# A hybrid mixer's convolution, recurrence and output projection in another order: one tile convolved by token halves, the gating by channel halves, the recurrence started one tile later

## The chip, the cores and the metric

One core of one Trainium2 chip runs the whole layer in a single program. The metric is the device time of one execution in microseconds (us). Before the change the median of three runs is 857.23 us (855.66 to 857.37). Five units of the core matter here: TensorE (PE in the rows; its weight loads are PEld) multiplies, VectorE (DVE), ScalarE (ACT) and GpSimd (POOL) work on elements, and SyncE (SP) issues most DMAs. Each works through its own list of instructions in order and waits where an input of the next instruction is not there.

## The reference

A decoder layer on 512 tokens of width 1024: a half-step feed-forward network, a mixer, another half-step feed-forward network, each behind an RMS norm and added to the stream. All is float32. The change lies in the mixer, which has a convolution branch (`u`) and a recurrence branch (`yr`) of 512 channels each:

```python
z = h @ w_in
c_val, c_gate, r_x, r_gate = jnp.split(z, [W_CONV, 2 * W_CONV, 2 * W_CONV + W_LRU], axis=-1)
u = c_val * jax.nn.sigmoid(c_gate)
u = causal_depthwise_conv(u, conv_dw, conv_dw_bias)          # 31 taps along the tokens
u = jax.nn.silu(layernorm(u, conv_ln_g, conv_ln_b))          # over the 512 channels
xr = causal_depthwise_conv(r_x, lru_conv_w, lru_conv_b)      # 4 taps
yr = rg_lru(xr, lru_w_a, lru_b_a, lru_w_x, lru_b_x, lru_lambda)
yr = yr * jax.nn.gelu(r_gate, approximate=True)
return jnp.concatenate([u, yr], axis=-1) @ w_out
```

In `rg_lru`, two sigmoid gates r and i are block-diagonal products of xr, a = exp(-8 r softplus(-lambda)), and h[t] = a[t] h[t-1] + sqrt(1 - a[t]^2) i[t] xr[t].

## The kernel before

Channels lie on the 128 partitions and the 512 tokens along the free axis, so each branch has four channel tiles, c = 0 to 3. To keep float32 accuracy, operands of the large products are split into a high and a low part (`hi`, `lo`), and each product takes three passes: hi by hi, hi by lo, lo by hi.

The kernel is a list of units, and each unit issues the matrix products of one weight slab. `run` walks through the list; after every 2.72 us of products it lets generators that stand beside the list (`chains`, `convs`, `pool_convs`) issue some of their steps, by a clock that it keeps in its head for each engine. A scheduler then orders each engine's instructions by priorities (`PR_CONV` is low, `PR_LN` high) and by the order in which they were issued. What it made stands fast: it is each engine's list.

The mixer's units, in order:

- `zc_units(c)`: gate and value columns of convolution tile c. `val_out` (L650) multiplies value by sigmoid(gate) and writes the input of the convolution. Tiles 0 and 1 come in two token halves, A (tokens 0 to 255) and B, tiles 2 and 3 whole. The order is 0A, 1A, 0B, 1B, tile 2, then `rx_units` (the recurrence's four input tiles, with their 4-tap convolution on VectorE at L775), then tile 3, then `rg_units` (the recurrence's four gate tiles; their Gelu at L799 waits for the key `roots`).
- The 31-tap convolution: tiles 0, 2 and 3 run on VectorE (`conv_dve`: 31 tap instructions into two PSUM accumulators and one addition, L691 to L701), tile 1 on GpSimd and ScalarE (`conv_pool`). `val_out` starts it when a tile's last token is there. Each finished tile adds a product with a matrix of ones to a bank `pm` (`channel_sum`, L677): the mean over channels. After the fourth, `layernorm` runs: subtraction of the mean (L731), squares (L736), a second `channel_sum` for the variance, square root (L740), reciprocal, scaling, Silu, split into `uhi` and `ulo` (L746 to L757).
- `lru`, the recurrence: eight float32 products `pga` with their sigmoids (L815, L816), tanh, exp and squares on ScalarE (L825 to L830), a VectorE step (L833), square roots and GpSimd products (L837, L838), four scans along the tokens (L845), then for both channel halves q = 0, 1 the product with the Gelu (L852), `yhi` (L853) and `ylo` (L854). It is started when the fourth `rx` tile is evacuated, and the gating waits until no VectorE convolution is left:

```python
            if c == 3:
                chains.append((PR_LRU, lru()))
```
```python
        while "gl" not in done or convs:
            yield 1
```

- `out_units`: the output projection. For each of four token tiles, 24 products with the `y` rows (`po<-hl,yhi` and `ylo`, L557 to L559), and after all of them the `u` rows. A unit for token tile 3 stands behind a wait for the variance.

Of the kernel before, what the change touches and what calls it, by code (L numbers as in the profile page):

```python
# [13 lines left out]
P = 128  # L14
# [61 lines left out]
def layer_kernel(ctx: ExitStack, tc, x, gains, w_g1, w_u1, w_d1a, w_d1b, w_in,  # L76
# [559 lines left out]
    def zc_units(c, parts):  # L636
# [12 lines left out]
        def val_out(t0, n):  # L649
            V.tensor_mul(mx["ub"][:, c, 30 + t0:30 + t0 + n], box["v"][:, :n], box["s"][:, :n])  # L650
            dve(0.7)
            if t0 + n == T:
                if c == 1:
                    pool_convs.append(conv_pool(c))
                else:
                    convs.append(conv_dve(c))
# [16 lines left out]
    def channel_sum(key, c, v):  # L673
        if key not in pm:
            pm[key] = [bank("pm"), 0]
        ps, n = pm[key]
        PE.matmul(ps, ones, v, start=n == 0, stop=n == 3)  # L677
        pm[key][1] += 1

    def conv_done(c):  # L680
        channel_sum("mean", c, conv_out(c))
        if pm["mean"][1] == 4:
            chains.append((PR_LN, layernorm()))


    def conv_dve(c):
        acc, o = [bank("pc"), bank("pc")], conv_out(c)
        for j in range(TAPS):
            src, to = mx["ub"][:, c, j:j + T], acc[j % 2]
# [6 lines left out]
            else:  # L696
                V.scalar_tensor_tensor(out=o if j == TAPS - 2 else to, in0=src,  # L697
                                       scalar=par(c, P_DW + j), in1=to,
                                       op0=ALU.mult, op1=ALU.add)
            yield 0.66  # L700
        V.tensor_add(o, acc[0], o)  # L701
        yield 0.66
        conv_done(c)
# [21 lines left out]
    def layernorm():  # L725
        mu = pm["mean"][0]
        sq = {}
        yield 1
        for c in range(4):
# [3 lines left out]
            if c % 2 == 0:  # L733
                sq[c // 2] = slot([P, 2, T], "sq")
            s = sq[c // 2][:, c % 2, :]
            S.activation(s, v, AF.Square)  # L736
            channel_sum("var", c, s)
        yield 1
        rs = sp.tile([P, T], F32, name=nm("rs"), tag="sg", bufs=2)
        S.activation(rs, pm["var"][0], AF.Sqrt, bias=lneps)  # L740
# [3 lines left out]
        half = [slice(0, HT), slice(HT, T)]  # L744
        for i, sl in enumerate(half):
# [8 lines left out]
        for i, sl in enumerate(half):  # L754
            for c in range(4):
                v, o = conv_out(c)[:, sl], hi[c // 2][:, c % 2, sl]
                V.tensor_sub(lo[c // 2][:, c % 2, sl], v, o.bitcast(F32))  # L757
            dve(1.6)
# [4 lines left out]
    def rx_units():  # L763
# [6 lines left out]
        def evac(c):  # L770
# [8 lines left out]
            if c == 3:  # L779
                chains.append((PR_LRU, lru()))  # L780
# [7 lines left out]
    def rg_units():  # L788
# [7 lines left out]
        def evac(c):  # L796
# [3 lines left out]
            if c == 3:  # L800
# [372 lines left out]
```

## Time and profile before

| | us |
|---|---|
| median of three runs | 857.23 (855.66 to 857.37) |
| the profiled execution | 858.1 |
| its span, first to last instruction | 856.1 |
| TensorE busy | 839.2 |
| VectorE busy | 636.7 |
| ScalarE busy | 424.7 |
| GpSimd busy | 89.5 |

The profile is of one execution; all times in rows are us from the start of its span. Where several instructions of one kind follow each other, a row of the timeline gives the first one's start, the time to the last one's end, and `xN` for their number; in brackets stands how long the engine was idle before, and what ended that. An instruction's own duration overlaps the start of the next, so the distance from start to start is the cost of one in a row of many. "Chain of waits" is the chain that ended last, followed back from the end. [...]

### The profile page before, as it was taken

What the parts mean: (1) busy time and instruction counts of PE and PEld (TensorE: products, weight loads), DVE (VectorE), ACT (ScalarE), POOL (GpSimd) and SP (SyncE); (2) the same over time, 40 slices, a digit from 0 to 9 for tenths busy, and PEclk for the clock granted to TensorE, in tenths of its full rate; (3) what the DMA queues carried; (4) which work ended last, traced back from release to release, by engine and by line L of the source; (5) the groups of instructions that cost most, each with busy time, mean ns of one, the idle gap of its engine ahead of it and who ended that gap; (6) DMA issues with size and microseconds to landing.
All of it is one profiled execution on the core that took longest, in us unless ns stands there. A gap on an engine that the chain in (4) does not pass through costs nothing.

```text
span 856.1 us, 13844 instructions
## 1 busy us (share of the span) xinstructions
PE 839.2 (98%) x5612; PEld 762.9 (89%) x5612; DVE 636.7 (74%) x899; ACT 424.7 (50%) x677; POOL 89.5 (10%) x112
## 2 busy tenths in 40 slices
PE   9999999999999999999995999999999999999996
PEld 8999988999889998998783889999889998899985
DVE  4989757998657983569988569896547994558844
ACT  6746534666425662435742535555215654136623
POOL 2000010000110001109820010000000000000001
PEclk9999999999999999999998999999999999999999
DMA  7547896555985569655451021334313335223302
GB/s 255 180 148 244 298 321 220 180 190 173 309 329 180 192 248 365 224 206 187 148 182 64 4 96 50 100 122 136 113 50 100 114 114 168 74 74 99 119 30 99
DMA packets 36723, 139.14 MB, mean 163 GB/s; under 512 B 5042, under 2 KB 5170, under 8 KB 33971
## 3 DMA queue, kind: packets, MB, share of 16 engines
q1 hardware_dynamic: 29170, 112.04, 38.5%
q0 software_dynamic: 6912, 25.17, 7.7%
q8 instruction: 44, 0.72, 0.4%
q10 hardware_dynamic: 576, 1.05, 0.3%
q14 instruction: 21, 0.16, 0.1%
HBM read 110.98 MB, written 27.26 MB: 161 GB/s over the span
## 4 chain that ended last, share of the span: by engine, by line
PE 93%; DVE 4%; ACT 1%; DMA 0%; issue 0%; POOLq 0%; SPq 0%; POOL 0%; ACTq 0%
PE px L331 25%; PE pz L331 12%; PE pd L557 8%; PE pd L558 8%; PE pd L559 8%; PE pz L316 7%; PE pw L331 6%; PE pgate L316 3%; PE pup L316 3%; DVE pc L697 2%; PE po L557 2%; PE po L558 2%; PE po L559 2%; PE ptr L369 1%; PE pdl L559 1%; PE pdl L558 1%
## 5 line engine op out<-in xcount | busy, mean ns | idle before, releaser
L215 DVE TENSOR_TENSOR hl<-raw,hl 128x1024 fp32r<-128x1024 f32 (+1 forms) x132 | 139.9, 1062 | 44.2 <-ACT hl L206 31.3
L215 DVE TENSOR_TENSOR hl<-tt,hl 128x1024 fp32r<-128x1024 f32 x78 | 95.0, 1217 | 32.8 <-ACT hl L242 19.0
L331 PE MATMUL px<-sx,hl 128*128 128x256 f32 x936 | 118.8, 276 | 0.0
L331 PE MATMUL pz<-sx,hl 128*128 128x256 f32 x936 | 118.8, 276 | 0.0
L557 PE MATMUL pd<-hl,act 128*128 128x512 f32 x304 | 118.6, 390 | 0.0
L558 PE MATMUL pd<-hl,act 128*128 128x512 f32 x304 | 118.4, 389 | 0.0
L559 PE MATMUL pd<-hl,act 128*128 128x512 f32 x304 | 118.3, 389 | 0.0
L331 PEld LDWEIGHTS px<-sx,hl 128*128 128x128 f32 x936 | 111.9, 188 | 0.0
L331 PEld LDWEIGHTS pz<-sx,hl 128*128 128x128 f32 x936 | 111.9, 188 | 0.0
L331 PE MATMUL px<-h_hi,hl 128*128 128x256 f32 x630 | 97.0, 277 | 0.0
L242 ACT CAST hl<-tt 128x1024 fp32r<-128x1024 f32 x78 | 81.9, 1052 | 24.5 <-PE pd L559 18.4
L331 PEld LDWEIGHTS px<-h_hi,hl 128*128 128x128 f32 x630 | 83.7, 188 | 1.4 <-DVE um L529 0.7
L242 ACT CAST hl<-raw 128x1024 fp32r<-128x1024 f32 x78 | 65.2, 836 | 37.1 <-PE pd L559 26.3
L206 ACT CAST hl<-raw 128x1024 fp32r<-128x1024 f32 x54 | 56.0, 1051 | 50.5 <-PE pd L559 39.7
L559 PEld LDWEIGHTS pd<-hl,act 128*128 128x128 f32 x304 | 57.1, 188 | 11.9
L558 PEld LDWEIGHTS pd<-hl,act 128*128 128x128 f32 x304 | 57.1, 188 | 11.5
L557 PEld LDWEIGHTS pd<-hl,act 128*128 128x128 f32 x304 | 57.1, 188 | 11.4
L316 PE MATMUL pz<-h_hi,hl 128*128 128x512 f32 (+2 forms) x322 | 64.8, 350 | 0.0
L316 PEld LDWEIGHTS pz<-h_hi,hl 128*128 128x128 f32 x322 | 51.7, 188 | 9.2 <-issue 1.9
L697 DVE SCALAR_TENSOR_TENSOR pc<-sx,ch,pc 128x512 f32<-128x512 f32 x84 | 56.9, 747 | 0.0
L300 DVE TENSOR_TENSOR slo<-sraw,shi 128x1024 fp32r<-128x1024 f32 x24 | 29.3, 1221 | 33.7 <-ACT shi L299 33.7
L299 ACT CAST shi<-sraw 128x1024 fp32r<-128x1024 f32 x24 | 25.3, 1052 | 49.0 <-DMA sraw<-in_w_in 26.0
(182 smaller groups left out, 1348.1 us busy)
## 6 DMA issues: line engine op xcount, KB each, us to landing
raw<-in_w_g SPq DMA_DIRECT2D x44, 512.0 KB, 3.4
raw<-in_w_u SPq DMA_DIRECT2D x44, 512.0 KB, 4.3
hl<-wsi SPq DMA_DIRECT2D x16, 1024.0 KB, 4.9
sraw<-in_w_in SPq DMA_DIRECT2D x16, 512.0 KB, 6.3
wsi<-shi POOLq DMA_DIRECT2D x16, 512.0 KB, 4.2
wsi<-slo POOLq DMA_DIRECT2D x16, 512.0 KB, 5.3
raw<-in_w_d1a SPq DMA_DIRECT2D x16, 512.0 KB, 4.6
raw<-in_w_d2a SPq DMA_DIRECT2D x16, 512.0 KB, 3.5
```

The source lines that it names most:

```text
L206: return S.copy(s.hi, s.raw)
L215: ins = V.tensor_sub(s.lo, s.raw, s.hi.bitcast(F32))
L242: S.copy(s.hi, s.raw)
L299: S.copy(hi, raws[-1])
L300: V.tensor_sub(lo, raws[-1], hi.bitcast(F32))
L316: ins = PE.matmul(ps[:, c0:c1], w[:, k, :], h[:, k, t0 + c0:t0 + c1], start=(i == 0 and k == 0), stop=(i == 2 and k == KT - 1))
L331: PE.matmul(ps[:, c0:c1], w[:, k * P:(k + 1) * P], h[:, k, c0:c1], start=(first and i == 0 and k == 0), stop=(i == 2 and k == 3), skip_gro ...
L369: ins = PE.transpose(pt[:, k, :], xs[0][:, (hf * 4 + k) * P:(hf * 4 + k + 1) * P], ident)
L557: PE.matmul(ps, ahi, whi, start=first, stop=False)
L558: PE.matmul(ps, ahi, wlo, start=False, stop=False)
L559: PE.matmul(ps, alo, whi, start=False, stop=last)
L697: V.scalar_tensor_tensor(out=o if j == TAPS - 2 else to, in0=src, scalar=par(c, P_DW + j), in1=to, op0=ALU.mult, op1=ALU.add)
```

## The change

It does four things.

- `conv_dve` takes a token range. Tile 0, which arrives in halves, is convolved half by half, in 64 instructions on 256 tokens in place of 32 on 512; it starts behind 0A in place of 0B. Tiles 2 and 3 stay whole.
- The mean over channels is no longer gathered tile by tile. GpSimd adds the first three tiles (two additions, L685 and L686), and `mean`, a unit of its own among the output projection's, issues two products with the matrix of ones in place of four.
- `lru` is started by `val_out` of convolution tile 3, behind the products of that tile, in place of by the fourth `rx` tile, ahead of them; more of its ScalarE work is kept in program order.
- The recurrence is scanned and gated by channel halves. For q = 0 and then q = 1: two scans, the product with the Gelu as soon as that half's Gelu is there, `yhi`, `ylo`. It no longer waits for the last convolution. `out_units` begins with the rows of half 0 for token tiles 0 and 1, then half 1 for tile 0, then `mean`, then half 1 for tile 1, then tile 2, the wait for the variance, tile 3.

```diff
         def val_out(t0, n):
...
-            if t0 + n == T:
-                if c == 1:
-                    pool_convs.append(conv_pool(c))
-                else:
-                    convs.append(conv_dve(c))
+            if c != 1:
+                convs.append(conv_dve(c, t0, n))
+            elif t0 + n == T:
+                pool_convs.append(conv_pool(c))
+            if c == 3:
+                chains.append((PR_LRU, lru()))
...
     def conv_done(c):
-        channel_sum("mean", c, conv_out(c))
-        if pm["mean"][1] == 4:
-            chains.append((PR_LN, layernorm()))
+        done["conv", c] = True
+        if c < 3 and all(("conv", i) in done for i in range(3)):
+            pm["s"] = slot([P, T], "cs")
+            G.tensor_add(pm["s"], conv_out(0), conv_out(2))
+            G.tensor_add(pm["s"], pm["s"], conv_out(1))
+
+    def mean():
+        need(("conv", 3))
+        pm["mean"] = channel_sum([pm["s"], conv_out(3)])
+        chains.append((PR_LN, layernorm()))
...
-    def conv_dve(c):
-        acc, o = [bank("pc"), bank("pc")], conv_out(c)
+    def conv_dve(c, t0, n):
+        if t0 == 0:
+            accs[c] = [bank("pc"), bank("pc")]
+        acc, o, at = accs[c], conv_out(c), slice(t0, t0 + n)
+        us = 0.66 if n == T else 0.42
         for j in range(TAPS):
-            src, to = mx["ub"][:, c, j:j + T], acc[j % 2]
+            src, to = mx["ub"][:, c, t0 + j:t0 + j + n], acc[j % 2][:, at]
...
-            if c == 3:
-                chains.append((PR_LRU, lru()))
...
-        for c in range(4):
-            at = (slice(None), c % 2, slice(None))
-            pin(V.tensor_tensor_scan(th[c // 2][at], r[c // 2][at], xr[c // 2][at],
-                                     0.0, ALU.mult, ALU.add))
-            dve(1.2)
-        while "gl" not in done or convs:
-            yield 1
         hi, lo = two("yhi", F32R), two("ylo", F32R)
         for q in range(2):
+            for c in (2 * q, 2 * q + 1):
+                at = (slice(None), c % 2, slice(None))
+                pin(V.tensor_tensor_scan(th[c // 2][at], r[c // 2][at], xr[c // 2][at],
+                                         0.0, ALU.mult, ALU.add))
+                dve(1.2)
+            while ("gl", 2 * q + 1) not in done:
+                yield 1
             pin(V.tensor_mul(th[q], th[q], lr["gl"][q]))
...
-        out_ = [Unit(sy, 5.44, lambda t=t: part((t,), sy, "y", True)) for t in range(3)]
+        out_ = [Unit(sy, 5.44, lambda: part((0, 1), sy, ("y", 0), True, (0, 1))),
+                Unit(sy, 2.72, lambda: part((0,), sy, ("y", 1), True, (2, 3))),
+                Unit([], 0.0, mean),
+                Unit(sy, 2.72, lambda: part((1,), sy, ("y", 1), True, (2, 3)))]
+        out_ += [Unit(sy, 2.72, lambda oh=oh: part((2,), sy, ("y", 1), True, halves=(oh,)))
+                 for oh in range(2)]
```

What it does to the engines' lists shows at three places. Line numbers of the changed kernel differ by some: L710 and L714 are its convolution taps and addition, L827 the `pga` products, L845 the VectorE step of the recurrence (L833 before), L859 the scans, L864 and L866 the gating and `ylo`.

TensorE, around the fourth convolution tile's value columns. Before, where `pz_4442` is that tile's gate and `pz_4512` its value:

```order
L316 MATMUL pz_4442<-h_hi,hl_4242 128x512 x8
L815 MATMUL pga_4473<-xr_4244,bd 128x512
L815 MATMUL pga_4476<-xr_4244,bd 128x512
L815 MATMUL pga_4479<-xr_4244,bd 128x512
L815 MATMUL pga_4482<-xr_4244,bd 128x512
L815 MATMUL pga_4489<-xr_4245,bd 128x512
L815 MATMUL pga_4492<-xr_4245,bd 128x512
L815 MATMUL pga_4495<-xr_4245,bd 128x512
L815 MATMUL pga_4498<-xr_4245,bd 128x512
L316 MATMUL pz_4512<-h_hi,hl_4292 128x512 x8
```

TensorE at the same place after, where `pz_4512` is the value of that tile again and `pz_4550` the recurrence's first gate tile:

```order
L316 MATMUL pz_4512<-h_hi,hl_4329 128x512 x8
L316 MATMUL pz_4550<-h_hi,hl_4376 128x512 x8
L316 MATMUL pz_4550<-h_lo,hl_4376 128x512 x8
L316 MATMUL pz_4550<-h_hi,hl_4376 128x512 x8
L827 MATMUL pga_4581<-xr_4275,bd 128x512
L827 MATMUL pga_4584<-xr_4275,bd 128x512
L827 MATMUL pga_4587<-xr_4275,bd 128x512
L827 MATMUL pga_4590<-xr_4275,bd 128x512
L827 MATMUL pga_4605<-xr_4276,bd 128x512
```

The recurrence's products have moved behind two more units. They stood ahead of the tile's value and now stand behind it and behind one gate tile.

VectorE, from the recurrence's step on `th` to the first taps of convolution tile 3. Before (`pc` are accumulators, `sx` the convolution's input):

```order
L701 TENSOR_TENSOR cv_4324<-pc_4322,cv_4324 128x512
L650 TENSOR_TENSOR sx_478_3865<-pz_4512,sgc_4508 128x512
L833 SCALAR_TENSOR_TENSOR th_4471<-i_4469,th_4471 128x1024
L833 SCALAR_TENSOR_TENSOR th_4472<-i_4470,th_4472 128x1024
L691 TENSOR_SCALAR pc_4627<-sx_478_3865,ch 128x512
L694 TENSOR_SCALAR pc_4628<-sx_478_3865,ch 128x512
L697 SCALAR_TENSOR_TENSOR pc_4627<-sx_478_3865,ch,pc_4627 128x512
```

After, where the rows around the step are taps of the same tile:

```order
L710 SCALAR_TENSOR_TENSOR pc_4602<-sx_478_3865,ch,pc_4602 128x512
L710 SCALAR_TENSOR_TENSOR pc_4601<-sx_478_3865,ch,pc_4601 128x512
L845 SCALAR_TENSOR_TENSOR th_4579<-i_4577,th_4579 128x1024
L845 SCALAR_TENSOR_TENSOR th_4580<-i_4578,th_4580 128x1024
L710 SCALAR_TENSOR_TENSOR pc_4602<-sx_478_3865,ch,pc_4602 128x512
L710 SCALAR_TENSOR_TENSOR pc_4601<-sx_478_3865,ch,pc_4601 128x512
```

Before, the step stood ahead of all 32 instructions of tile 3's convolution. Now 17 of them stand ahead of it, and 11 taps behind it before the first scan.

VectorE, at the end of the last convolution. Before (`L701` is its last addition, `gl` the Gelu, `pm` the mean):

```order
L697 SCALAR_TENSOR_TENSOR pc_4627<-sx_478_3865,ch,pc_4627 128x512
L701 TENSOR_TENSOR cv_4324<-pc_4627,cv_4324 128x512
L852 TENSOR_TENSOR th_4471<-th_4471,gl_4563 128x1024
L854 TENSOR_TENSOR ylo_4747<-th_4471,yhi_4745 128x1024
L731 TENSOR_TENSOR cv_4103<-cv_4103,pm_4320 128x512 x2
L731 TENSOR_TENSOR cv_4324<-cv_4324,pm_4320 128x512 x2
L852 TENSOR_TENSOR th_4472<-th_4472,gl_4564 128x1024
L854 TENSOR_TENSOR ylo_4748<-th_4472,yhi_4746 128x1024
```

After:

```order
L859 SCALAR_TENSOR_TENSOR th_4579<-r_4575,xr_4275 128x512 x2
L710 SCALAR_TENSOR_TENSOR pc_4602<-sx_478_3865,ch,pc_4602 128x512
L864 TENSOR_TENSOR th_4579<-th_4579,gl_4548 128x1024
L710 SCALAR_TENSOR_TENSOR pc_4602<-sx_478_3865,ch,pc_4602 128x512
L710 SCALAR_TENSOR_TENSOR cv_4317<-sx_478_3865,ch,pc_4602 128x512
L866 TENSOR_TENSOR ylo_4744<-th_4579,yhi_4742 128x1024
L859 SCALAR_TENSOR_TENSOR th_4580<-r_4576,xr_4276 128x512 x2
L714 TENSOR_TENSOR cv_4317<-pc_4601,cv_4317 128x512
L864 TENSOR_TENSOR th_4580<-th_4580,gl_4549 128x1024
L866 TENSOR_TENSOR ylo_4745<-th_4580,yhi_4743 128x1024
L744 TENSOR_TENSOR cv_3990<-cv_3990,pm_4826 128x512 x2
```

The gating of half 0 has moved ahead of the last taps, the scans of half 1 stand behind it, and both gatings now stand ahead of the subtraction of the mean.

## Rows read from the trace of the kernel before

**Rows 1.** The page: TensorE's busy time, share of the span and instructions; then the shares of the span in the chain of waits, by engine.

```profile
PE 839.2 (98%) x5612; PEld 762.9 (89%) x5612; DVE 636.7 (74%) x899; ACT 424.7 (50%) x677; POOL 89.5 (10%) x112
...
PE 93%; DVE 4%; ACT 1%; DMA 0%; issue 0%; POOLq 0%; SPq 0%; POOL 0%; ACTq 0%
```

**Rows 2.** Windows around the one gap of TensorE: the stretch and its length, then busy us of PE, PEld, DVE, ACT and POOL with their instructions, the granted clock, the DMA share and GB/s.

```profile
456.00:459.50 3.50, 0.00 (x0) 0.00 (x0) 3.47 (x7) 0.00 (x0) 0.00 (x0) 0.74 0.16 66
459.50:462.00 2.50, 2.33 (x3) 0.76 (x4) 1.39 (x2) 1.04 (x1) 0.00 (x0) 0.50 0.00 0
462.00:464.70 2.70, 2.70 (x7) 1.98 (x8) 2.70 (x5) 0.00 (x0) 0.00 (x0) 0.53 0.00 0
464.70:467.60 2.90, 1.35 (x6) 0.75 (x5) 1.78 (x3) 1.03 (x2) 0.00 (x0) 1.00 0.00 0
```

**Rows 3.** The chain of waits in the mixer, in order of time: start, us, engine, output and line.

```profile
399.37 0.86 PE pm L677 x2
...
443.63 13.81 DVE pc L697 x21
...
459.49 1.14 DVE th L852
460.65 1.05 ACT yhi L853
```

**Rows 4.** Timeline of TensorE in the mixer: start, us, engine, line, operation, output<-input, form, number. A float32 product such as `pga` or `pm` counts as two instructions.

```profile
416.44 7.03 PE L815 MATMUL pga<-xr,bd 128*128 128x512 f32 x16
...
449.63 1.52 PE L316 MATMUL pz<-h_hi,hl 128*128 128x512 f32 x6
450.99 1.02 PE L677 MATMUL pm<-cv,ones 128*128 128x512 f32 x2
...
459.54 2.07 PE L677 MATMUL pm<-cv,ones 128*128 128x512 f32 x2 [7.06 <-DVE cv L701]
461.75 0.79 PE L557 MATMUL po<-hl,yhi 128*128 128x512 f32 x1
...
464.47 0.44 PE L559 MATMUL po<-hl,ylo 128*128 128x512 f32 x1
...
467.66 0.50 PE L557 MATMUL po<-hl,yhi 128*128 128x512 f32 x1 [1.61 <-ACT yhi L853]
...
468.46 3.60 PE L677 MATMUL pm<-sq,ones 128*128 128x512 f32 x8
...
488.02 0.39 PE L559 MATMUL po<-hl,ylo 128*128 128x512 f32 x1
...
490.06 0.39 PE L559 MATMUL po<-hl,ylo 128*128 128x512 f32 x1
490.29 0.39 PE L557 MATMUL po<-hl,uhi 128*128 128x512 f32 x1
```

**Rows 5.** Timeline of VectorE in the mixer, the same columns.

```profile
366.62 0.42 DVE L650 TENSOR_TENSOR sx<-pz,sgc 128x256 f32<-128x256 f32 x1 [1.36 <-PE pz L316]
372.25 0.43 DVE L650 TENSOR_TENSOR sx<-pz,sgc 128x256 f32<-128x256 f32 x1 [5.21 <-PE pz L316]
...
388.60 0.69 DVE L650 TENSOR_TENSOR sx<-pz,sgc 128x512 f32<-128x512 f32 x1 [0.92 <-PE pz L316]
...
429.05 0.69 DVE L650 TENSOR_TENSOR sx<-pz,sgc 128x512 f32<-128x512 f32 x1 [2.50 <-PE pz L316]
431.00 2.36 DVE L833 SCALAR_TENSOR_TENSOR th<-i,th 128x1024 f32<-128x1024 f32 x2 [1.27 <-ACT i L830]
433.28 0.81 DVE L691 TENSOR_SCALAR pc<-sx,ch 128x512 f32<-128x512 f32 x1
...
438.60 5.03 DVE L845 TENSOR_TENSOR_SCAN th<-r,xr 128x512 f32<-128x512 f32 x4
443.55 13.89 DVE L697 SCALAR_TENSOR_TENSOR pc<-sx,ch,pc 128x512 f32<-128x512 f32 x21
...
461.73 1.23 DVE L854 TENSOR_TENSOR ylo<-th,yhi 128x1024 fp32r<-128x1024 f32 x1 [1.11 <-ACT yhi L853]
462.87 2.48 DVE L731 TENSOR_TENSOR cv<-cv,pm 128x512 f32<-128x512 f32 x4
```

**Rows 6.** Timeline of ScalarE in the recurrence and the norm, the same columns.

```profile
423.62 0.69 ACT L816 ACTIVATE i<-pga,ch 128x512 f32<-128x512 f32 x1
424.19 1.95 ACT L825 ACTIVATE th<-r,psp 128x512 f32<-128x512 f32 x3
...
427.46 2.56 ACT L828 ACTIVATE r<-r,nsp 128x512 f32<-128x512 f32 x4
429.93 1.99 ACT L830 ACTIVATE i<-r 128x1024 f32<-128x1024 f32 x2
...
467.52 2.19 ACT L736 ACTIVATE sq<-cv 128x512 f32<-128x512 f32 x4
...
472.09 0.69 ACT L740 ACTIVATE rs<-pm,lneps 128x512 f32<-128x512 f32 x1 [1.09 <-PE pm L677]
```

**Rows 7.** Timeline of VectorE in the norm's last steps, the same columns.

```profile
476.10 2.70 DVE L750 TENSOR_TENSOR cv<-cv,rs 128x256 f32<-128x256 f32 x8
479.26 0.76 DVE L757 TENSOR_TENSOR ulo<-cv,uhi 128x256 fp32r<-128x256 f32 x2 [0.46 <-ACT uhi L752]
```

**Rows 8.** Timeline of GpSimd: the recurrence's products with the square roots.

```profile
434.43 4.76 POOL L838 TENSOR_TENSOR xr<-xr,th 128x1024 f32<-128x1024 f32 x2 [5.79 <-ACT th L837]
```

More of the change, by code (lines that the diff above doesn't have):

```diff
@@ L670, in conv_out, with channel_sum @@
         return cv.setdefault(c // 2, slot([P, 2, T], "cv"))[:, c % 2, :]
[L673 to L678, printed above, removed]
-    def conv_done(c):
-        channel_sum("mean", c, conv_out(c))
-        if pm["mean"][1] == 4:
-            chains.append((PR_LN, layernorm()))
-    def conv_dve(c):
-        acc, o = [bank("pc"), bank("pc")], conv_out(c)
+    def channel_sum(vs):
+        ps = bank("pm")
+        for i, v in enumerate(vs):
+            PE.matmul(ps, ones, v, start=i == 0, stop=i == len(vs) - 1)
+        return ps
+    def conv_done(c):
+        done["conv", c] = True
[7 more added lines that the diff above has]
+        chains.append((PR_LN, layernorm()))
+    accs = {}
+    def conv_dve(c, t0, n):
[3 more added lines that the diff above has]
+        us = 0.66 if n == T else 0.42
         for j in range(TAPS):
-            src, to = mx["ub"][:, c, j:j + T], acc[j % 2]
+            src, to = mx["ub"][:, c, t0 + j:t0 + j + n], acc[j % 2][:, at]
             if j == 0:
@@ L725, in layernorm @@
     def layernorm():
-        mu = pm["mean"][0]
-        sq = {}
-        yield 1
+        mu = pm["mean"]
+        sq = [slot([P, 2, T], "sq") for _ in range(2)]
         for c in range(4):
@@ L732, in layernorm @@
             dve(0.69)
[L733 to L737, printed above, removed]
+            S.activation(sq[c // 2][:, c % 2, :], v, AF.Square)
         yield 1
+        var = channel_sum([sq[c // 2][:, c % 2, :] for c in range(4)])
         rs = sp.tile([P, T], F32, name=nm("rs"), tag="sg", bufs=2)
-        S.activation(rs, pm["var"][0], AF.Sqrt, bias=lneps)
+        S.activation(rs, var, AF.Sqrt, bias=lneps)
         done["var"] = True
@@ L744, in layernorm, with low @@
         half = [slice(0, HT), slice(HT, T)]
+        def low(sl):
+            for c in range(4):
+                v, o = conv_out(c)[:, sl], hi[c // 2][:, c % 2, sl]
+                V.tensor_sub(lo[c // 2][:, c % 2, sl], v, o.bitcast(F32))
+            dve(1.6)
         for i, sl in enumerate(half):
@@ L753, in layernorm @@
             dve(1.6)
-        for i, sl in enumerate(half):
-            for c in range(4):
-                v, o = conv_out(c)[:, sl], hi[c // 2][:, c % 2, sl]
-                V.tensor_sub(lo[c // 2][:, c % 2, sl], v, o.bitcast(F32))
-            dve(1.6)
+            if i:
+                low(half[0])
+        low(half[1])
         done["u"] = (hi, lo)
@@ L799, in evac @@
                 S.activation(lr["gl"][c // 2][:, c % 2, :], lr["g", c], AF.Gelu_apprx_tanh))
[L800 to L801 removed]
+            done["gl", c] = True
         out_ = []
@@ L855, in lru @@
             dve(2.4)
-        done["y"] = (hi, lo)
+            done["y", q] = (hi, lo)
     def out_units(after):
@@ L875, in part @@
             for t in ts if first else ():
-                box[t] = [bank("po") for _ in range(2)]
+                if t not in box:
+                    box[t] = [bank("po") for _ in range(2)]
             for t in ts:
```

22 lines of the change are left out of this document (10 added, 12 removed).

## The prediction

> **What bounds the kernel now.** I read the page first. TensorE is busy 98% of the span and holds 93% of the chain of waits [rows 1], so only a stretch in which it stands still, runs slowly or does needless products can give time. [...] The timeline gives the pieces [rows 4]. The input products end with the six at 449.63, a mean product and two more, at about 452.4. TensorE then waits 7.06 us for the last convolution's addition, does the last mean product in 2.07 us at half clock, starts the `y` products at 461.75 with the recurrence's half 0, stops again for 1.61 us before half 1, and from 467.66 runs on. The `u` products begin at 490.29. Nothing of the list behind that is reordered, so I follow the start of the `u` products and carry its shift to the end.
>
> What TensorE waits for is VectorE. In the chain stand 21 taps in 13.81 us, so 0.658 us each, and then the gating [rows 3]. VectorE itself was late because it had waited: 5.21 us for tile 0's second half at 372.25, 0.92 us at 388.60, and 2.50 and 1.27 us around 429 to 431, where it needed the fourth tile and then the recurrence's squares [rows 5].
>
> **The change, part by part.**
>
> *Mean.* Each of the four mean products costs TensorE 0.86 us [rows 3]. The first three stand among the input products before the seam, so these end 3 x 0.9 = 2.7 us earlier (0.9 with the break in the stream), at 449.65. After the change two mean products (1.75 us) stand among the `y` products, where TensorE has no cover. Two are saved for good, 1.75 us. GpSimd's two additions of the first three tiles fall behind tile 2's convolution, at 425, and are needed 40 us later; GpSimd had 5.79 us without work before 434.43 [rows 8].
>
> *Recurrence one tile later.* The eight `pga` products began at 416.44 [rows 4]. Without one mean product that place in the list comes at 415.5; now the tile's value (5.44 us a unit) and one gate tile go first, so `pga` begins at 415.5 + 10.9 = 426.4. From there I keep the distances of the trace. First `pga` to the VectorE step on `th` was 431.00 - 416.44 = 14.56 [rows 4, 5]; one tanh more now stands behind the last sigmoid (0.61 us), where one was slipped in between [rows 6]. So the step starts at 426.4 + 15.1 = 441.5.
>
> *Tile 0 by halves.* No instruction of this kind with 256 elements is in the trace. From below: the 256-wide product in SBUF costs 0.34 (2.70 us for eight) where the 512-wide one costs 0.60 [rows 5, 7]; from above: the tap of 512, 0.658. A tap adds the same fixed part to 256 elements that it adds to 512, and the elements differ by 0.26, so I take 0.40, nearest to the lower row. The 64 cost 25.6 us against 21.1 for 32, or 4.5 more, but start about 11 us earlier and fill the waits at 366.62 and 372.25. At 388.60 VectorE has ten half taps and an addition left of tile 0 where it had nine taps and an addition, so it leads by 6.6 - 4.4 = 2.2 us. Tile 2's convolution ended at 429.05 - 2.50 = 426.55 [rows 5]; it now ends at 426.55 - 2.2 + 0.7 = 425.0, with the tile 3 product (0.69 us) moved in front of its last five instructions. The fourth tile is there at 421.2 and costs a wait of no more than 1 us. Then 17 of tile 3's instructions take 11.8 us with the first four taps on one accumulator, so VectorE stands before the `th` step at 436.9 and **waits 4.6 us** for squares that come at 441.5. Behind it queue all that TensorE needs: the last taps, the scans and the gating. The halving's lead therefore ends in this wait and is worth nothing by my sum; in turn it may cost 4.6 us more without harm.
>
> [...]
>
> *Gating between the last taps.* From 441.5: two steps 2.28 us (431.00 to 433.28), 11 taps 7.24, two scans 2.47 (half of 438.60 to 443.55), one tap 0.66, and from the gating's start to the first `y` product 461.75 - 459.40 = 2.35 [rows 4, 5]. The first `y` product of half 0 starts at **456.5**, against 461.75. The square roots and GpSimd's products fit beside the 11 taps (they took some 6 us from 433.3 on [rows 8]). Half 1 follows behind a gating (1.14), two taps (1.32), `ylo` (1.23), two scans (2.47) and the addition (0.65): its first product can start at 454.15 + 6.8 + 2.35 = 463.3, its `ylo` at 464.5. Half 0 for token tiles 0 and 1 is 24 products. TensorE has stood still from 449.65 to 456.5, 6.85 us against 7.06, so I let the clock fall as before and stay low as long as from 459.54 to 464.7: 5.2 us for 12 products, then 12 at 0.227 (nine between 488.02 and 490.06 [rows 4]), which ends at 464.4. Half 1 is just there, so **the second stop goes**.
>
> *Tail.* 12 products (2.72) to 467.15, the mean (1.75) to 468.9, 13 products to 471.9, four variance products (3.45, as 8 x 0.43) to 475.35. The subtraction of the mean begins at 468.95, the squares 0.7 us behind it, so the fourth is done by 472.1 and the variance does not wait. Of 96 `y` products 47 remain: 10.65 us. The `u` products begin at **486.1**, against 490.29: 4.2 us earlier. Their first `ulo` was there 7.55 us after the square root's start (472.09 to 479.64 [rows 6, 7]); 475.4 + 7.55 = 482.9 leaves 3 us.
>
> By the pieces: stops and half clock shrink by 2.4 us, two mean products are 1.75.
>
> The profiled execution is 858.1, its span 856.1, and 2.0 lie around it. The sum is 858.1 - 4.2 = 853.9 for such an execution. It stood 0.9 above the median of the runs, so the median goes from 857.23 to **853.0**.
>
> **The rivals.**
>
> *The mean comes too late* (855.4). It ends at 468.9 where it ended at 461.6, and the variance products stand in the middle of TensorE's list, so squares that are late stop everything. Before, the squares began 4.65 us after the subtraction (462.87 and 467.52 [rows 5, 6]), since ScalarE stood behind the second `yhi`. With that distance the variance would end at 477.75, 2.4 us later, and 1.8 us of gain would be left. Against it: in the new list both gatings and both `yhi` stand ahead of the subtraction.
>
> *Half taps cost near a whole one, and the kernel gets slower* (859 to 863). The place is tile 0's convolution: at 0.60 us the 64 are 12.8 us dearer than taken. The 0.9 us at 388.60, 1 us at the fourth tile and the 4.6 us at the `th` step absorb 6.5; the rest, 6.3, stands against a gain of 4.2, so 859.3, and at the upper bound, 0.658, 863.0. It decides from 0.40 + 10.7/64 = 0.57 us on. The 256-wide rows speak against it [rows 5, 7]. [...]
>
> *The halving does pay* (849). If the recurrence's ScalarE part were done sooner than the 15.1 us that I copy, up to 4.6 us of VectorE's wait would go. The sigmoids follow eight products of 0.86 us and four tanh, a table, four exp and a square follow them in the trace without slack [rows 6], so I see nothing that shortens it.
>
> *The clock behaves otherwise* (852.6 to 855.0). If it does not fall in the shorter stop, half 0 ends sooner but half 1 is only there at 463.3 to 464.5, which gives 0.4 us. If it stays low for twice as long, 2 us are lost.
>
> **How the numbers follow.** The forecast, 853.0, with 851.5 to 854.8 of its own, has 0.66. A late mean or a clock low for longer, 855 to 856, has 0.17; both sides of 855.5 share it. Dear half taps or another wait that ends slower, 859.3 to 863.0, have 0.07. The halving that pays, 848.5 to 851, has 0.06. No effect at all has 0.04. The range of 8 in 10 is 851.0 to 856.2. A measurement of this kernel can tell about 0.2%, 1.7 us, from no change: faster than 855.5 has 0.80, within 0.2% 0.13, slower 0.07.
>
> **What would show it.** Right: the first `y` product 6 to 7.5 us behind the last input product, no second stop, VectorE idle 4 to 5 us before the `th` step with ScalarE's squares ending it, the `u` products 4 us earlier. The step on the halves is wrong if VectorE does not wait there or half taps are over 0.5 us apart. The tail is wrong if TensorE stops before the variance products or the first `u` product. The forecast falls if `pga` does not begin 10 us later than before.

## The result, and the profile after

The changed kernel takes 850.88 us (median of 4 runs, 850.63 to 852.47), the kernel before 856.44 (median of 4, 855.59 to 857.37): a ratio of 0.9933, 95% interval 0.9919 to 0.9946. Forecast were 853.0 and 851.0 to 856.2, so the sign is right and the time lies 0.12 us under the low end. The profiled execution of the changed kernel took 851.07 us, its span 849.2. Two later executions of the kernel before, of 1055.22 and 2184.69 us, stand far outside all others and are in none of the numbers below.

The page of the changed kernel, its rows for TensorE and the chain [rows 1]:

```profile
PE 833.4 (98%) x5608; PEld 759.6 (89%) x5608; DVE 640.5 (75%) x931; ACT 425.0 (50%) x677; POOL 91.3 (11%) x114
...
PE 94%; DVE 2%; ACT 1%; DMA 1%; SPq 0%; issue 0%; POOLq 0%; POOL 0%; ACTq 0%
```

The windows of the changed kernel around TensorE's gap, with the columns of [rows 2]:

```profile
450.00:453.80 3.80, 0.00 (x0) 0.00 (x0) 3.76 (x5) 0.97 (x2) 0.00 (x0) 0.76 0.39 166
453.80:456.50 2.70, 2.57 (x6) 1.71 (x7) 2.70 (x4) 0.57 (x2) 0.00 (x0) 0.50 0.00 0
456.50:458.60 2.10, 2.10 (x7) 1.62 (x6) 2.10 (x4) 0.00 (x0) 0.00 (x0) 0.50 0.00 0
458.60:461.00 2.40, 2.40 (x12) 1.97 (x11) 1.28 (x2) 1.05 (x1) 0.00 (x0) 0.96 0.00 0
```

At the seam between the mixer's input products and its output projection one stop is left, and behind it one stretch in which the granted clock is 0.50 of full speed (0.50 to 0.53 before [rows 2]). After it, nothing stops before the `u` products.

The timeline of TensorE in the changed kernel [rows 4]:

```profile
47.82 0.74 PE L331 MATMUL px<-h_hi,hl 128*128 128x256 f32 x5
...
424.11 7.03 PE L827 MATMUL pga<-xr,bd 128*128 128x512 f32 x16
...
445.51 1.97 PE L316 MATMUL pz<-h_hi,hl 128*128 128x512 f32 x8
453.93 0.80 PE L557 MATMUL po<-hl,yhi 128*128 128x512 f32 x1 [6.45 <-ACT yhi L865]
...
458.59 0.48 PE L558 MATMUL po<-hl,yhi 128*128 128x512 f32 x1
...
464.62 1.02 PE L677 MATMUL pm<-cs,ones 128*128 128x512 f32 x2
...
469.34 3.59 PE L677 MATMUL pm<-sq,ones 128*128 128x512 f32 x8
...
483.44 0.39 PE L557 MATMUL po<-hl,uhi 128*128 128x512 f32 x1
```

Its timeline of VectorE [rows 5], with 18 half taps, tile 0's last long row, first:

```profile
377.68 7.14 DVE L710 SCALAR_TENSOR_TENSOR pc<-sx,ch,pc 128x256 f32<-128x256 f32 x18
...
427.61 0.75 DVE L707 TENSOR_SCALAR pc<-sx,ch 128x512 f32<-128x512 f32 x1 [0.74 <-ACT r L828]
...
439.17 2.36 DVE L845 SCALAR_TENSOR_TENSOR th<-i,th 128x1024 f32<-128x1024 f32 x2 [3.58 <-ACT i L842]
441.45 7.33 DVE L710 SCALAR_TENSOR_TENSOR pc<-sx,ch,pc 128x512 f32<-128x512 f32 x11
448.70 2.33 DVE L859 TENSOR_TENSOR_SCAN th<-r,xr 128x512 f32<-128x512 f32 x2
450.95 0.73 DVE L710 SCALAR_TENSOR_TENSOR pc<-sx,ch,pc 128x512 f32<-128x512 f32 x1
451.58 1.22 DVE L864 TENSOR_TENSOR th<-th,gl 128x1024 f32<-128x1024 f32 x1
...
466.54 2.48 DVE L744 TENSOR_TENSOR cv<-cv,pm 128x512 f32<-128x512 f32 x4 [4.85 <-PE pm L677]
```

The chain of waits [rows 3] now runs through the recurrence, not through the convolution:

```profile
424.27 6.88 PE pga L827 x16
...
434.33 1.28 ACT L840
435.63 1.39 ACT r L840 x3
...
438.19 0.96 ACT i L842
439.15 0.02 issue
439.17 2.36 DVE th L845 x2
441.54 7.25 DVE pc L710 x11
448.79 2.24 DVE th L859 x2
```

ScalarE and GpSimd at the two joints that were in doubt: the squares of the norm begin 0.78 us behind the subtraction [rows 6], and GpSimd's sum of three tiles is there 39 us before its product [rows 8].

```profile
467.32 2.36 ACT L746 ACTIVATE sq<-cv 128x512 f32<-128x512 f32 x4 [6.89 <-DVE cv L744]
```

```profile
424.48 1.27 POOL L686 TENSOR_TENSOR cs<-cs,cv 128x512 f32<-128x512 f32 x1
```

Both kernels have the same products from the first `px` product, at some 48 us in the first feed-forward network, to the mixer. From there to the first `u` product the kernel before needs 490.29 - 50.14 = 440.15 us, the changed one 483.44 - 47.82 = 435.62: **4.53 us less in the mixer**. From the `u` products to the end both need the same, 365.81 and 365.76. The remaining 2.3 us of the 6.9 between the spans lie ahead of `px`, where the lists are alike. I use this distance (from the first `px` to the first `u` product) below, since it leaves the start-up out.

### The profile page after: what moved, and what is told of

It is laid out like the page before. It is cut to its first block, busy times and chain, and to the rows that moved or that the text cites. A ratio compares the mean times of both kernels' runs of the same rounds, so it can differ in the third digit from the quotient of the medians.

```text
span 849.2 us, 13877 instructions
## 1 busy us (share of the span) xinstructions
PE 833.4 (98%) x5608; PEld 759.6 (89%) x5608; DVE 640.5 (75%) x931; ACT 425.0 (50%) x677; POOL 91.3 (11%) x114
## 3 DMA queue, kind: packets, MB, share of 16 engines
q10 hardware_dynamic: 576, 1.05, 0.3%
## 4 chain that ended last, share of the span: by engine, by line
PE 94%; DVE 2%; ACT 1%; DMA 1%; SPq 0%; issue 0%; POOLq 0%; POOL 0%; ACTq 0%
PE px L331 25%; PE pz L331 12%; PE pz L316 8%; PE pd L557 8%; PE pd L558 8%; PE pd L559 8%; PE pw L331 6%; PE pgate L316 3%; PE pup L316 3%; PE po L557 2%; PE po L559 2%; PE po L558 2%; PE pdl L559 1%; PE pdl L557 1%; PE pdl L558 1%; DMA xt<-in_x 1%
## 5 line engine op out<-in xcount | busy, mean ns | idle before, releaser
L316 PE MATMUL pz<-h_hi,hl 128*128 128x512 f32 (+2 forms) x322 | 63.0, 346 | 0.0
L710 DVE SCALAR_TENSOR_TENSOR pc<-sx,ch,pc 128x256 f32<-128x256 f32 (+1 forms) x112 | 61.4, 615 | 0.1
L331 PE MATMUL px<-h_lo,hl 128*128 128x256 f32 x312 | 48.2, 277 | 0.0
```

What stands on the lines that cost most here:

```text
L316: ins = PE.matmul(ps[:, c0:c1], w[:, k, :], h[:, k, t0 + c0:t0 + c1], start=(i == 0 and k == 0), stop=(i == 2 and k == KT - 1))
L331: PE.matmul(ps[:, c0:c1], w[:, k * P:(k + 1) * P], h[:, k, c0:c1], start=(first and i == 0 and k == 0), stop=(i == 2 and k == 3), skip_gro ...
L710: V.scalar_tensor_tensor(out=o[:, at] if j == TAPS - 2 else to, in0=src, scalar=par(c, P_DW + j), in1=to, op0=ALU.mult, op1=ALU.add)
```

## The experiments

### The start-up: chance, or the change?

First rows of four executions. Kernel before, the profile from which the prediction was made: its first products behind some idle ones, `g` (two products, which the rows count as four instructions), and the first `px` product:

```profile
4.48 3.78 PE L941 MATMUL g<-grow,warm 1*128 1x512 f32 x4
...
14.75 1.29 PE L316 MATMUL pgate<-h_hi,hl 128*128 128x256 f32 x9
...
50.14 0.74 PE L331 MATMUL px<-h_hi,hl 128*128 128x256 f32 x5
```

Changed kernel, the same rows (its `px` is above):

```profile
4.33 2.20 PE L959 MATMUL g<-grow,warm 1*128 1x512 f32 x4
...
11.10 1.29 PE L316 MATMUL pgate<-h_hi,hl 128*128 128x256 f32 x9
```

I ran both kernels again, unchanged.

> The changed kernel once more, unchanged. In the first profiles the changed kernel gained 4.54 us in the mixer and 2.31 us in its first 48 us, where both kernels have the same instructions in the same order; there the matrix products ran at half rate until about 11.1 us instead of 14.7. Theory A: the start-up has two lengths, about 2 us apart, in either kernel and whatever the change. Then these runs fall into two groups, near 850.8 and near 852.5 us, and the profile, whichever group it is from, shows its first `u` product 4.5 us earlier than before when both are counted from the first `px` product. Rival B: the change itself shortens the start-up. Then every run is at 851.1 or below, and the first `px` product stands near 47.8.

> The kernel before once more, unchanged. Theory A (two lengths of the start-up in either kernel): two groups, near 855.6 and near 857.3 us; where the profile is from the short one, its first `px` product stands near 47.8 and the span is about 854; where it is from the long one, near 50.1 and 856. Rival B (the start-up of this kernel is long and the change shortens it): the first `px` product stands near 50.1 in every profile of it, and no profile shows 47.8.

Changed: 850.67 to 853.58 in 6 runs, half of them below 851.3 and half above 852.3; distance 435.63. Before: 12 runs, six from 855.40 to 855.73, six from 857.29 to 858.11; distance 440.16. The groups are in both kernels, but the profile of the kernel before was again a long one, that of the changed one a short one. A second repeat:

> The changed kernel once more, unchanged, for a profile of its long start-up. Theory A: times in two groups, near 850.8 and near 852.6 us; a profile with `g` products of 3.78 us has its time in the upper group, its first `px` product near 49.4 to 50.1, and the distance from there to the first `u` product is 435.6. Rival B (the change shortens the start-up): no profile of this kernel shows 3.78.

> The kernel before once more, unchanged, for a profile of its short start-up. Theory A: a profile with `g` products near 2.1 us has a time near 855.5, its first `px` product near 47.5, and 440.15 us from there to the first `u` product. Rival B (this kernel always starts long): no profile of it shows `g` near 2.1.

The same picture (changed a short start, 435.58; before a long one, 440.16), so B was still alive. A third, with one more profile of each:

> The kernel before, unchanged, for its start-up. Theory A (either length in either kernel): about one profile in two has `g` products near 2.1 us, its first `px` product near 47.6 and a time near 855.5. Rival B: `g` at 3.78 and `px` at 49.4 to 50.2 again.

> The changed kernel, unchanged, for its start-up. Theory A (either length in either kernel): about one profile in two has `g` products of 3.78 us, its first `px` product at 49.4 to 50.1 and a time near 852.6. Rival B: `g` near 2.1 and `px` near 47.6 again.

The kernel before with the short start, 855.46 us:

```profile
4.33 2.06 PE L941 MATMUL g<-grow,warm 1*128 1x512 f32 x4
...
47.60 0.74 PE L331 MATMUL px<-h_hi,hl 128*128 128x256 f32 x5
...
487.67 0.39 PE L557 MATMUL po<-hl,uhi 128*128 128x512 f32 x1
```

The changed kernel with the long one, 852.53 us:

```profile
4.54 3.77 PE L959 MATMUL g<-grow,warm 1*128 1x512 f32 x4
...
49.56 0.74 PE L331 MATMUL px<-h_hi,hl 128*128 128x256 f32 x5
...
459.48 0.42 PE L559 MATMUL po<-hl,ylo 128*128 128x512 f32 x1
...
484.73 0.39 PE L557 MATMUL po<-hl,uhi 128*128 128x512 f32 x1
```

B falls: each kernel has both starts. The fourth repeat gave a long one of before (857.99, distance 440.16) and a short one of the changed kernel (850.63, 435.41). Over all runs the kernel before has 29 different times below 856.4 with median 855.52, and 51 between 857.1 and 858.2 with median 857.65; the changed one 10 with median 850.76 and 10 with 852.74 (one of them, 849.14, stands alone). Like against like the gain is 4.8 us (short) and 4.9 (long).

The distance is not quite fixed either. Five profiles of the kernel before have 440.07 to 440.16, five of the changed one 435.17 to 435.63; the 435.17 is that of the long start just shown. In the four of them whose rows at the stop are on record, the first `y` product stands 406.06 to 406.12 behind `px`. What differs is how long the products behind the stop stay slow, at 0.61 to 0.80 us in place of 0.39 (the granted clock is 0.50 there in the windows of the first profile): eight `y` products and 3.8 us in the profile with 435.17 (until 459.48), ten and 4.7 us in the first one (until 458.59). So a difference of 0.2 or 0.4 in one distance of a kernel with this stop is no more than that.

Does more running ahead of the `g` products make the start short?

```diff
-IDLE = (7, 3, 3, 3)
+IDLE = (14, 3, 3, 3)
```

> As the changed kernel, but 28 idle products instead of 14 stand ahead of the first products of the program. In the start-up the first products after the idle ones ran at full rate in two profiles of the changed kernel (four `g` in 2.08 and 2.20 us) and at half rate in both of the kernel before (3.78). Theory A: the length of the start-up is chance, in either kernel; more idle products at the start delay the work by up to 3.4 us, and times still fall into groups about 2 us apart, 851 to 856 us. Rival C: what is missing is more running ahead of the `g` products; then all `g` run at full rate, and the times stand in one group at 851 to 852.5.

All `g` ran at full rate in its profile (1.98 us), as rival C says; but this profile (850.93) is of the lower group, where theory A has full rate too, so it does not decide. The six times do: they still fall into two groups, 850.65 to 850.94 and 852.89 to 853.37, as theory A says. More idle products cost nothing here and don't remove the groups.

The rate of `g` alone does not make the length of the start. In the kernel with the gating behind the last convolution (below) `g` took 2.25 us, then TensorE waited 1.67 us and ran slower (eight `ptr` products in 1.68 us, where the eight before had taken 1.30; granted clock 0.67 from 10 to 15 us), and `px` came at 49.15, between the short starts (47.5 to 47.8) and the long ones (49.4 to 50.1):

```profile
10.92 1.68 PE L369 MATMUL ptr<-ident,xn 128*128 128x128 f32 x8 [1.67 <-DVE xn L359]
```

### The parts of the change, undone one at a time

**The recurrence at the fourth `rx` tile again**, all else as changed:

```diff
             elif t0 + n == T:
                 pool_convs.append(conv_pool(c))
-            if c == 3:
-                chains.append((PR_LRU, lru()))
...
                                        op0=ALU.mult, op1=ALU.add)
                 dve(0.69)
+            if c == 3:
+                chains.append((PR_LRU, lru()))
```

> As the changed kernel, but the recurrence is started at the fourth `rx` tile as before the change, ahead of the value product of convolution tile 3: this part of the change alone is undone. Theory: the later start of the recurrence is a cost that the rest of the change pays for. `pga` comes about 11 us earlier than in the changed kernel, TensorE finds the first half of `y` when its input products end, the stop and the half clock go: 842.5 to 844 us. Rival 1, the later start is what lets the half convolution and the gating through: slower than the changed kernel, 852 to 855. Rival 2, VectorE's sum of work is the bound in either place: within 1 us of the kernel with the recurrence behind the value product.

```profile
49.44 0.74 PE L331 MATMUL px<-h_hi,hl 128*128 128x256 f32 x5
...
447.06 1.98 PE L316 MATMUL pz<-h_hi,hl 128*128 128x512 f32 x8
448.88 0.39 PE L557 MATMUL po<-hl,yhi 128*128 128x512 f32 x1
...
477.36 0.39 PE L557 MATMUL po<-hl,uhi 128*128 128x512 f32 x1
```

844.08 us (843.13 to 845.04), ratio 0.9854 (0.9837 to 0.9871), distance 427.92: 7.7 us less than the changed kernel. The first `y` product follows the input products at once at 448.88 and the granted clock stays at 1.00 there (446 to 462 us), as the theory says. The later start of the recurrence is the change's cost, not its gain: the other parts together bring 440.15 - 427.92 = 12.2 us, and this one takes 7.7 of them back.

**Recurrence behind the tile's value, but with its products issued at once:**

```diff
             if c == 3:
                 chains.append((PR_LRU, lru()))
+                step_chains()
+                step_chains()
```

> As the changed kernel, but the recurrence's steps are issued at once behind the value product of convolution tile 3, so that its eight `pga` products stand ahead of the first gate tile instead of behind it. Theory: what VectorE waits for before the step on `th`, and TensorE at the seam, is the late `pga`; 5.44 us earlier they start near 418.7 (changed kernel's time), the step near 433.8, the first `y` product no longer stands behind a stop (the input products end near 447.3 and half 0 is there by then), the clock does not fall, and the first `u` product comes about 8 us earlier: 842 to 844 us. Rival 1, that starting the recurrence later is what helps (its ScalarE and VectorE work would again hold the convolution back): 851 us or more. Rival 2, that VectorE's work is the bound and only the wait of 3.6 us goes: 847 to 848.

847.27 us (847.16 to 847.29), ratio 0.9891 (0.9875 to 0.9906), distance 429.46. `pga` and the step on `th` came 5.4 us earlier, counted from `px`, the long stop and the lower clock went as the theory says (0.44 us and a granted clock of 1.00 from 446 to 462 us), but it missed the size: the number is rival 2's. What the theory had not counted is VectorE's two first scans, which took twice what they take in the changed kernel (4.52 for 2.33), beside GpSimd; that GpSimd is the cause is put to the test in the last experiment. VectorE and GpSimd in this kernel:

```profile
441.68 4.52 DVE L861 TENSOR_TENSOR_SCAN th<-r,xr 128x512 f32<-128x512 f32 x2
```

```profile
439.24 4.76 POOL L852 TENSOR_TENSOR xr<-xr,th 128x1024 f32<-128x1024 f32 x2 [4.35 <-ACT th L851]
```

**Tile 0 whole**, all else as changed:

```diff
-            if c != 1:
-                convs.append(conv_dve(c, t0, n))
-            elif t0 + n == T:
-                pool_convs.append(conv_pool(c))
+            if t0 + n == T:
+                if c != 1:
+                    convs.append(conv_dve(c, 0, T))
+                else:
+                    pool_convs.append(conv_pool(c))
```

> As the changed kernel, but tile 0 is convolved whole again (32 instructions on 512 tokens, started behind its second half). To be read by the distance from the first `px` product to the first `u` product, 435.6 us in two profiles of the changed kernel and 440.15 in two of the kernel before. Theory (the prediction's): VectorE's lead from the halves ends in its 3.58 us wait for the recurrence's squares, so the wait before the step on `th` shrinks to about 1.5 to 2.5 us, the step starts at the same distance from `pga`, and the distance is 435.1 to 435.8. Rival: the halving pays, and without it the distance is 437.8 or more (2.2 us of lead lost); the time then goes up by as much.

Distance 484.43 - 49.63 = 434.80, below the theory's 435.1, so the halves don't pay in this kernel; they cost 0.4 to 0.8 us. 851.79 us (850.41 to 852.32). VectorE's waits are not the 1.5 to 2.5 us that were expected but 2.52, ahead of tile 3's first instruction, and 2.86; the step keeps its place:

```profile
426.19 0.69 DVE L715 TENSOR_TENSOR cv<-pc,cv 128x512 f32<-128x512 f32 x1
429.40 0.81 DVE L705 TENSOR_SCALAR pc<-sx,ch 128x512 f32<-128x512 f32 x1 [2.52 <-ACT r L829]
...
440.97 2.36 DVE L846 SCALAR_TENSOR_TENSOR th<-i,th 128x1024 f32<-128x1024 f32 x2 [2.86 <-ACT i L843]
```

440.97 - 49.63 = 391.34, where the changed kernel has 439.17 - 47.82 = 391.35. The lead of the halves is there: tile 2's addition stands at 426.19 - 49.63 = 376.56, in the changed kernel, whose row follows, at 422.29 - 47.82 = 374.47, 2.1 us earlier. It ends in these waits.

```profile
422.29 0.69 DVE L714 TENSOR_TENSOR cv<-pc,cv 128x512 f32<-128x512 f32 x1
```

Behind the step, ten taps instead of 11 then stand ahead of the scans, and the first `y` product is 0.68 us earlier: one tap. So what the halves cost here is a place in the list.

**Tile 0 whole and the recurrence at the fourth `rx` tile**, both edits together:

> Both undone: the recurrence starts at the fourth `rx` tile as before the change, and tile 0 is convolved whole; mean, gating and scans by halves stay. With the early recurrence alone undone VectorE waited 4.54 us for the fourth tile's value, and the first half of `y` was ready 5 us before TensorE wanted it. Theory: the 2.2 us of lead that the halves gave end in that wait, and the distance from the first `px` to the first `u` product stays at 427.9 within 0.5 us. Rival: with the recurrence early VectorE is the bound at the seam, so that the halves pay: 429.5 to 430.5.

846.97 us (845.28 to 847.49), distance 429.86, 1.94 more than with halves. The number is the rival's. VectorE gets the fourth tile at the same time in both (427.40 and 427.39), so the lead does end in that wait; what differs lies behind it. With the halves two taps fill the wait ahead of the step on `th`; whole, it waits 1.27 us there. And the first two scans run beside GpSimd, whose sums of tiles have slipped between its products:

```profile
429.36 2.36 DVE L846 SCALAR_TENSOR_TENSOR th<-i,th 128x1024 f32<-128x1024 f32 x2 [1.27 <-ACT i L843]
...
436.96 5.09 DVE L860 TENSOR_TENSOR_SCAN th<-r,xr 128x512 f32<-128x512 f32 x2
```

5.09 against 3.25, and 1.27: 3.1 us of VectorE, of which 2.9 show at the end of the last convolution (its addition at 463.98 against 461.10).

**The mean tile by tile** (four products, three of them among the input products):

```diff
-        if c < 3 and all(("conv", i) in done for i in range(3)):
-            pm["s"] = slot([P, T], "cs")
-            G.tensor_add(pm["s"], conv_out(0), conv_out(2))
-            G.tensor_add(pm["s"], pm["s"], conv_out(1))
+        if c < 3:
+            if "mean" not in pm:
+                pm["mean"], pm["n"] = bank("pm"), 0
+            PE.matmul(pm["mean"], ones, conv_out(c), start=pm["n"] == 0, stop=False)
+            pm["n"] += 1
...
-        pm["mean"] = channel_sum([pm["s"], conv_out(3)])
+        PE.matmul(pm["mean"], ones, conv_out(3), start=False, stop=True)
```

> As the changed kernel, but the mean is gathered tile by tile again in four products with the matrix of ones, three of them among the input products, one among the `y` products; GpSimd's two additions go. Theory (the prediction's): three products at 0.86 to 0.9 us ahead of the seam make the recurrence and all behind it later by 1.8 to 2.6 us, and one product of 0.86 fewer stands among the `y` products, so the distance from the first `px` to the first `u` product is 436.5 to 437.4 where the changed kernel has 435.6. Rival: the mean products ahead of the seam lie beside TensorE's stop and cost nothing, one product fewer behind it saves 0.86: 434.8 to 435.6.

855.11 us (851.82 to 855.6), distance 487.75 - 50.12 = 437.63, 2.0 more than changed: the theory's sign, 0.2 above its range, which is within what the length of the slow stretch makes (13 `y` products in 5.9 us here). **The gating behind the last convolution:**

```diff
-            while ("gl", 2 * q + 1) not in done:
+            while ("gl", 2 * q + 1) not in done or convs:
                 yield 1
```

> As the changed kernel, but the gating waits until the last convolution has been issued, as before the change; scans by halves stay. The two last taps and the addition then stand ahead of the first half's gating (1.97 us), where they stood behind it. Theory: the first `y` product comes 1.9 to 2.1 us later, the stop of TensorE grows from 6.45 to 8.4 us, and the distance from the first `px` to the first `u` product is 437.5 to 437.8 where the changed kernel has 435.6. Rival: half 1 is what counts (it comes no later, since the same work stands ahead of it), TensorE makes the difference good, and the distance stays within 0.5 us of 435.6.

855.24 us (853.39 to 856.46), distance 487.07 - 49.15 = 437.92, 2.3 more than changed; TensorE's stop is 8.76 us. The theory holds, 0.1 above its range. The three instructions cost 2.30 us instead of 1.97. The last three taps and the addition start 0.77 to 0.78 us apart (from 452.30 to 454.63), and not 0.66 as the taps in the long rows (11 in 7.33 us); each of them reads what the one before has just written, and that this makes the difference is my reading, which no run shows by itself.

The times of these last two kernels do not fall into two groups as clearly (851.82 and then 854.18 to 855.6; 853.39 to 856.46).

The parts undone one by one do not add up to the gain: 2.0 and 2.3 for the mean and the gating, less 0.4 to 0.8 for the halves and 7.7 for the later recurrence, would be a loss of some 4 us, where the change gains 4.5. What a part is worth depends on where the recurrence starts: the halves cost up to 0.8 us with the late start and bring 1.94 with the early one. The mean and the gating were not undone with the early start, and the scans by halves not by themselves, so what each of these brings there is not shown.

### A scan beside GpSimd

```diff
-SCAN_LATER = 5
+SCAN_LATER = 7
```

`SCAN_LATER` is the number of steps that the recurrence's generator lets pass before it issues the scans. The rest is the kernel with the recurrence at the fourth `rx` tile.

> As the kernel with the recurrence at the fourth `rx` tile (427.92 us from the first `px` to the first `u` product), but the first two scans stand behind more taps of the last convolution, at about 441 us, where GpSimd's products (432.73 to 437.5) are over. In that kernel the first two scans took 3.25 us, the later two 2.33; with the recurrence behind the value product the first two took 4.52, with tile 0 whole 5.09, each time while GpSimd worked. Theory: a scan of VectorE is stretched while GpSimd works, so here the first two take 2.3, the last convolution ends 0.9 us earlier, the second half of `y` comes sooner, and the distance is 426.6 to 427.3. Rival: the first two scans are long for another reason, and stay at 3 us or more; the later first half brings a wait for TensorE, 428 or more.

Distance 476.81 - 49.94 = 426.87, and the scans:

```profile
432.33 9.97 DVE L708 SCALAR_TENSOR_TENSOR pc<-sx,ch,pc 128x512 f32<-128x512 f32 x15
442.21 2.33 DVE L859 TENSOR_TENSOR_SCAN th<-r,xr 128x512 f32<-128x512 f32 x2
```

The theory holds. TensorE has no stop at the seam any more. 844.36 us (844.05 to 844.47), ratio 0.9856 (0.9842 to 0.987): against 844.08 for the kernel without the delay that shows no difference in the medians, since that one had two short starts in four (843.13 and 843.32; long 844.83 and 845.04); in the distance it is 1.05 us better. Both beat the changed kernel by some 8 us, like start against like.

## Why the prediction was right, and where it was wrong

**The step that failed** is the last of the sum: "It stood 0.9 above the median of the runs, so the median goes from 857.23 to 853.0." I took the three times as one value with noise. They were two values, 2.1 us apart: by their times, 857.23 and 857.37 were long starts, 855.66 a short one. Three of the four runs measured are short starts, again by their times, so the base to subtract from was 855.52 and not 857.23. That is 1.7 of the 2.1 us between 853.0 and 850.88; the rest is the gain, put at 4.2, which the groups give as 4.8. Either alone would have left the median within my range (855.52 - 4.2 = 851.3; 857.23 - 4.8 = 852.4). A range for both starts would have reached from 851.3 down by the 1.5 us that the forecast's own range had below it, to 849.8.

**The gain, 4.2, measured 4.53** in the distance of the first profiles. The mechanism held: every step of the table is there, within 0.4 us. Counted from `px` in the clock of the profile before (2.32 us on the rows after), step by step:

| | forecast | measured |
|---|---|---|
| `pga` starts | 426.4 | 426.43 |
| VectorE's waits between the fourth tile and `th` | 4.6 | 0.74 + 3.58 |
| step on `th` | 441.5 | 441.49 |
| first `y` product | 456.5 | 456.25 |
| TensorE's stop | 6.85 | 6.45 |
| first `u` product | 486.1 | 485.76 |

- *Mean.* Right: three products fewer ahead of the seam. Left out of the changed kernel, it costs 2.0 us. The rival of the late mean fell: the squares began 0.78 us behind the subtraction, and the variance products did not wait.
- *Recurrence later.* Place and time right to 0.03 us. I had priced it as part of the sum, not by itself; undone, it gives 7.7 us. The 4.6 us wait that I named was its visible end. Of it, 3.58 us stood at the step, less than the 4 to 5 that I had named as a sign; 0.74 stood 12 instructions ahead, where the second accumulator waits for ScalarE's sigmoid of a `pga` product. The code takes the banks of both from one pool, so I read this as a wait for the bank; no run shows it by itself.
- *Halves.* 0.40 us a half tap, as taken (18 in 7.14 us), 0.26 less than a whole one (0.66). The rival of dear half taps fell. So did the one that the halving pays: without it the kernel is 0.4 to 0.8 us faster. The lead of 2.2 us that ends in the wait was right (2.1).
- *Gating.* Two scans took 2.25 us from start to start, not 2.47. I had halved the four of [rows 5], whose first ran beside the last 0.6 us of GpSimd's product [rows 8]. That is 0.22 of the 0.33 missing; another 0.1 is a slip of the sum, since 475.35 + 10.65 is 486.0 and not 486.1.
- *Clock.* It fell again, and ten products ran at 0.50 until 458.59, 4.7 us, where I had copied 5.2 for 12. That this came near was partly luck: in another execution of the same kernel it lasted 3.8 us. The second stop went.

Left open: what sets the length of the start-up and of the lower clock behind the stop, which these runs show and do not explain. With both varying, the gain in the distance is 4.4 to 5.0 us from profile to profile, and the 4.8 and 4.9 of the groups lie within it.

## What to carry to other kernels

Look at the single times before a median is taken as the base: with two groups, say which group the profiled execution is from, and let the range hold both. A work item that is moved for one reason has a cost of its own, so undo it alone: in the kernel as changed two parts gain 2 us each, one costs up to 0.8, and the later recurrence costs 7.7. Do not add such figures up; here they give the wrong sign. See what GpSimd does where a scan is placed: beside its product two scans took 3.25 us here, some 5 us later, behind it, 2.33.

## What the runs showed of the hardware that I had not expected

- **The start-up has two rates in the same code.** The two `g` products take 3.77 to 3.78 us or 1.98 to 2.25, about half and full rate. What stands ahead is alike: TensorE's idle products run from 1.04 us on, and `g` starts at 4.33 in a long start (the second profile of the kernel before, 3.78) as in a short one (the first of the changed kernel, 2.20). In the long start the half rate lasts until about 12 to 14 us. In some of the short ones it comes back: eight `ptr` products take 1.77 at 7.31 in the short start of the kernel before, against 1.24 in the first profile of the changed kernel. In the second profile of the changed kernel, where they take 1.72 at 7.21, the granted-clock column shows 0.80 from 5 to 10 us and 0.86 from 10 to 15. But it shows 1.00 for the first 15 us of the profile before although products ran at half rate, so there the durations are to be read. The two groups of times, 2.1 us apart in the kernel before and 2.0 in the changed one, go with the start: short in every profile of the lower group, long in every profile of the upper one, of both kernels. What decides between them no run shows.
- **A scan takes longer beside GpSimd.** Two scans take 2.33 us by themselves; 3.25 with some 1.06 us of GpSimd's product beside them, 4.52 with 2.3 us, 5.09 with some 4 us, in which GpSimd's own addition was held up as well and took 2.21 instead of 1.30 (the row below). In the first two the scans lost nearly all of the time they shared, 0.92 of 1.06 and 2.19 of 2.32. Taps in the same place are not slower (15 in 9.97 us, 0.66 each, with GpSimd busy for 4.77 of it). Why the scan is held up and the tap is not, no run shows.

```profile
438.76 2.21 POOL L685 TENSOR_TENSOR cs<-cs,cv 128x512 f32<-128x512 f32 x1
```
